# State-space mixer of an encoder block: plain fp32 products and VectorE power tables in place of split operands and GpSimd

## The chip, the cores and the metric

The kernel runs on one core of a Trainium2 chip. The metric is the device time of one launch in microseconds (us). The core has five engines with an instruction queue each: TensorE (PE; its weight loads are listed as PEld), VectorE (DVE), ScalarE (ACT), GpSimd (POOL) and SyncE (SP), which here only issues DMAs.

## The reference, cut to what matters

The program is one encoder block: RMSNorm, an input projection into a Fourier branch, a state-space branch and two gate vectors, a merge, and a mixture of experts. The change touches the state-space branch alone. For 32 groups of 16 channels and both directions it computes, with 64 complex states per group:

```
    lam = lax.complex(a_re.astype(jnp.float32), a_im.astype(jnp.float32))
    dt = jnp.exp(log_dt.astype(jnp.float32))[:, None]
    a_bar = jnp.exp(lam * dt)
    b_mat = lax.complex(b_re.astype(jnp.float32), b_im.astype(jnp.float32))
    b_bar = ((a_bar - 1.0) / lam)[..., None] * b_mat
    bu = jnp.einsum('blgc,gnc->blgn', ug.astype(jnp.complex64), b_bar)
    a = jnp.broadcast_to(a_bar, bu.shape)
    _, h = lax.associative_scan(_scan_combine, (a, bu), axis=1, reverse=reverse)
    c_mat = lax.complex(c_re.astype(jnp.float32), c_im.astype(jnp.float32))
    return jnp.einsum('blgn,gcn->blgc', h, c_mat).real
...
    y = y.reshape(b, l, SSM_WIDTH) + d_skip.astype(jnp.float32) * uf
    y = jax.nn.gelu(y)
```

The rest of the block is the same in both kernels.

## The kernel before, in words

The program runs in stages: input projection (`stage_a`), Fourier branch (`stage_f`), gates with the state-space branch (`stage_s`), merge and routing (`stage_m`), experts (`stage_e`) and a last sum (`stage_z`). This document is about `stage_s`.

The 2048 positions are cut into 256 blocks of 8. Within a block the recurrence is written as matrix products; from block to block a scan carries the state. The 32 groups are handled in 16 chunks of two groups (`CG = 2`), and a chunk `c` passes these steps:

- `prep(c)` builds `win`, the products of the input matrix `bb` with eight powers of the transition (`pw_w`); `prep_cy(c)` builds `cy` from the output matrix `cc` and powers `pw_c`; `prep_tab(c)` builds `tab`, a table of 256 rotations, as the product of two tables of 16. All three are complex outer products. In the kernel before they are done by `cmulp` (L599 to L605) on GpSimd: two multiplications (L602, L603), a subtraction (L604) and an addition (L605) for each group.
- `kern(c)` transposes `win` on TensorE (L986) into PSUM and splits it (`winT`).
- `toeplitz(c)` makes the kernel of the block in PSUM (L998 to L1001), ACT copies it out and sends it through DRAM (`kd`); `load_toep(c)` reads it back as a Toeplitz matrix (`toep`).
- `states(c)` multiplies `winT` with the input `u` into `ps` (L1026), and ACT copies the result to `sx` (L1029).
- `scan(c)`, on VectorE: rotate (L1041 to L1044), four scans over 256 blocks (L1048), rotate back (L1049 to L1052).
- `enter(c)` puts the scanned states, shifted by one block, into `hs`.
- `result(c)` sums three products in PSUM (`py`): `toep` with `u`, and two of `cy` with `hs`. The moving `hs` is read with a step of two elements (`"p (c h) -> p h c"`).
- `gelu(c)`: L1077 to L1093 and two stores.

A product with split operands is `mm3` (L56 to L61): each operand is a high part and a low part in the reduced fp32 format (`fp32r`), and three matmuls add high by high, low by high and high by low. `split` (L50 to L54) makes the parts: a cast on ACT (L53) and a subtraction on VectorE, or on GpSimd for `cyp` (L54).

The gate products fill TensorE between the steps. There are 64 gate units; a unit is 24 matmuls of 512 columns (`pg`, eight times `mm3`), a Tanh on ACT (L831), in half of the units a VectorE instruction (L833), and a store (L836). The Python generator `gates` emits a unit at every `g(1)`, and `split_w` makes the weights' parts (`wg_h` on ACT, `wg_l` on VectorE) some units ahead. The order of instructions on each engine is the order in which the code is written (the schedule is manual), so an engine's queue is in order: an instruction that waits holds up everything behind it. SyncE issues loads and stores in the same fashion. `gt_t`, the tile that takes a gate unit out of PSUM, has two buffers, so a unit's Tanh needs the store of the unit before last to have landed.

The loop over chunks (L1129 to L1155) runs, for chunk `c`: `states(c+1)`, `scan(c+1)`, one gate unit, `result(c)`, `kern(c+2)`, the split of `u`, `toeplitz(c+1)`, the first part of `gelu(c)`, `prep(c+3)`, one gate unit, the split and the building of `cy`, `load_toep(c+1)`, `enter(c+1)`, the rest of `gelu(c)`, `prep_tab(c+3)`, and the remaining gate units (one or two). With 16 chunks it takes most of the stage.

Of the kernel before, what the change touches and what calls it, by code (L numbers as in the profile page):

```python
# [36 lines left out]
class K:  # L37
# [640 lines left out]
    def ssm_setup(self, tp):  # L678
# [80 lines left out]
        A.copy(self.pw_w[f], pw[f, :, 0:8])  # L759
        A.copy(self.pw_w[r], pw[r, :, 7::-1])  # L760
        A.copy(self.pw_c[f], pw[f, :, 1:9])
        A.copy(self.pw_c[r], pw[r, :, 8:0:-1])
# [113 lines left out]
    def stage_s(self):  # L876
# [61 lines left out]

        def prep(c):
# [9 lines left out]
            win = s["win"] = p1.tile([P, 2, CG, 8, 16], F32, name="win")  # L949

            def weights(o, pw, m):
                tw = [t[:, :, :, 0:128].rearrange("p q g (s c) -> p q g s c", s=8) for t in temps()]
                for g in range(CG):
                    a = m[:, :, CG * c + g].unsqueeze(2).to_broadcast([P, 2, 8, 16])
                    w = tuple(pw[:, q : q + 1, :, CG * c + g].unsqueeze(3).to_broadcast([P, 2, 8, 16]) for q in range(2))
                    self.cmulp(GP, o[:, :, g], a, w, tuple(t[:, :, g] for t in tw))
# [4 lines left out]
        def prep_tab(c):
            if c >= N:
                return
            s = st[c]
            tr = [t.rearrange("p q g (a b) -> p q g a b", a=16) for t in temps()]
            tab = s["tab"] = p2.tile([P, 2, CG, 256], F32, name="tab")
            for g in range(CG):
                a = self.rot[0][:, :, CG * c + g].unsqueeze(2).to_broadcast([P, 2, 16, 16])
                w = tuple(self.rot[1][:, q : q + 1, CG * c + g].unsqueeze(3).to_broadcast([P, 2, 16, 16]) for q in range(2))
                self.cmulp(GP, tab[:, :, g].rearrange("p q (a b) -> p q a b", a=16), a, w, tuple(t[:, :, g] for t in tr))  # L970

        def prep_cy(c):
            if c < N:
                cy = st[c]["cy"] = p1.tile([P, 2, CG, 8, 16], F32, name="cy")
                st[c]["weights"](cy, self.pw_c, self.cc)

        def kern(c):
# [4 lines left out]
            winT = s["winT"] = self.pair(p1, [P, 2, CG, P], "winT")
            pk = psk.tile([P, 2, CG, P], F32, name="pw", tag="pk")
            for q in range(2):
                for g in range(CG):
                    nc.tensor.transpose(pk[:, q, g], s["win"][:, q, g].rearrange("p s c -> p (s c)"), self.ident)  # L986
# [1231 lines left out]
```

## Time and profile before

| what | us |
|---|---|
| median of 3 runs | 2553.9 (2549.96 to 2554.51) |
| the profiled execution, its own time | 2549.1 |
| span of the profiled execution | 2547.2 |
| PE busy in the span | 2328.8 (91%) |
| DVE busy | 2188.3 (86%) |
| ACT busy | 1389.3 (55%) |
| POOL busy | 1240.8 (49%) |

How to read it: times are us from the start of the span. "Busy" for PE counts matmuls to their modelled ends, which overlap the next matmul's start, so the pace of matmuls is read from start to start. The state-space chunks run from about 330 to 785 us of the span; the experts take the second half of the program, from about 1240 us on. In the rows, `m` stands for the tiles `m1` and `m2`, `u` and `toep` for `u0` and `toep0`.

### The profile page before, as it was taken

What the parts mean: (1) busy time and instruction counts of PE and PEld (TensorE: products, weight loads), DVE (VectorE), ACT (ScalarE), POOL (GpSimd) and SP (SyncE); (2) the same over time, 40 slices, a digit from 0 to 9 for tenths busy, and PEclk for the clock granted to TensorE, in tenths of its full rate; (3) what the DMA queues carried; (4) which work ended last, traced back from release to release, by engine and by line L of the source; (5) the groups of instructions that cost most, each with busy time, mean ns of one, the idle gap of its engine ahead of it and who ended that gap; (6) DMA issues with size and microseconds to landing.
All of it is one profiled execution on the core that took longest, in us unless ns stands there. A gap on an engine that the chain in (4) does not pass through costs nothing.

```text
span 2547.2 us, 33067 instructions
## 1 busy us (share of the span) xinstructions
PE 2328.8 (91%) x11930; PEld 1935.9 (76%) x11930; DVE 2188.3 (86%) x2816; ACT 1389.3 (55%) x1680; POOL 1240.8 (49%) x755
## 2 busy tenths in 40 slices
PE   6998988998899899999799997999999999999974
PEld 6996766777778799997677776777777777777752
DVE  7776699998993645556799998999999999999998
ACT  4443344544444322222577775777777777777731
POOL 2223898999960200012332462256565565655434
PEclk9999999999999999999799998999999999999985
DMA  5566624253335533326799988999999999989982
GB/s 193 183 195 236 222 88 142 79 187 120 118 97 157 180 109 100 116 76 231 257 335 374 366 314 351 369 355 350 356 354 369 363 360 378 375 339 344 359 324 115
DMA packets 201409, 632.75 MB, mean 248 GB/s; under 512 B 28998, under 2 KB 99656, under 8 KB 150556
## 3 DMA queue, kind: packets, MB, share of 16 engines
q1 hardware_dynamic: 170668, 571.01, 62.0%
q0 software_dynamic: 23104, 47.06, 4.9%
q10 hardware_dynamic: 7472, 12.55, 1.6%
q8 instruction: 94, 1.54, 0.2%
q14 instruction: 71, 0.58, 0.1%
HBM read 560.75 MB, written 103.32 MB: 261 GB/s over the span
## 4 chain that ended last, share of the span: by engine, by line
DVE 43%; PE 25%; issue 13%; POOL 11%; DMA 4%; ACT 2%; SPq 1%; DVEq 0%; POOLq 0%; ACTq 0%
DVE w_l L1715 21%; POOL t4a L602 3%; DVE xn L1853 3%; DVE xT_l L1794 3%; POOL t4b L603 3%; PE po L59 2%; PE po L61 2%; PE po L60 2%; DVE xg L1819 2%; DVE a L1893 2%; DVE aT_l L1794 1%; DVE a L1864 1%; PE pg L61 1%; PE pg L59 1%; PE pg L60 1%
## 5 line engine op out<-in xcount | busy, mean ns | idle before, releaser
L1715 DVE TENSOR_TENSOR w_l<-raw,w_h 128x2048 fp32r<-128x2048 f32 x384 | 868.5, 2292 | 12.7 <-ACT w_h L1709 12.7
L1709 ACT CAST w_h<-raw 128x2048 fp32r<-128x2048 f32 x384 | 726.4, 1906 | 206.4 <-PE pgu L61 162.1
L59 PE MATMUL pgu<-w_h,xT_h 128*128 128x512 f32 x1024 | 407.8, 398 | 14.0 <-issue 14.0
L60 PE MATMUL pgu<-w_l,xT_h 128*128 128x512 f32 x1024 | 408.4, 399 | 5.0 <-DVE w_l L1715 2.3
L61 PE MATMUL pgu<-w_h,xT_l 128*128 128x512 f32 x1024 | 402.7, 393 | 0.0
L1782 POOL DMA_INDIRECT y<-xg,ix x42 | 221.6, 5276 | 363.1 <-DVE aT_l L1794 326.0
L60 PEld LDWEIGHTS pgu<-w_l,xT_h 128*128 128x128 f32 x1024 | 194.2, 190 | 65.3 <-DVE w_l L1715 28.2
L59 PEld LDWEIGHTS pgu<-w_h,xT_h 128*128 128x128 f32 x1024 | 194.4, 190 | 53.6 <-issue 14.2
L61 PEld LDWEIGHTS pgu<-w_h,xT_l 128*128 128x128 f32 x1024 | 194.1, 190 | 39.7 <-DVE xT_l L1794 0.2
L1782 POOL DMA_INDIRECT y<-x_l,ix x22 | 114.9, 5221 | 205.6 <-DVE aT_l L1794 198.1
L61 PE MATMUL pg<-hk_h,wg_l 128*128 128x512 f32 x512 | 204.3, 399 | 10.3 <-DVE wg_l L54 10.3
L59 PE MATMUL pg<-hk_h,wg_h 128*128 128x512 f32 x512 | 207.6, 405 | 3.5 <-ACT gt_t L831 3.1
L59 PE MATMUL py<-w_h,aT_h 128*128 128x512 f32 x512 | 205.6, 402 | 4.0 <-ACT aT_h L1792 4.0
L60 PE MATMUL pg<-hk_l,wg_h 128*128 128x512 f32 x512 | 204.6, 400 | 0.0
L61 PE MATMUL py<-w_h,aT_l 128*128 128x512 f32 x512 | 200.4, 391 | 0.0
L60 PE MATMUL py<-w_l,aT_h 128*128 128x512 f32 x512 | 200.2, 391 | 0.0
L1777 POOL DMA_INDIRECT xg<-x,ix x42 | 176.1, 4193 | 12.8 <-issue 12.8
L1353 POOL TENSOR_TENSOR inv<-mv,mhalf 128x1 f32<-128x1 f32 x16 | 9.0, 560 | 239.3 <-DVE mv L1352 239.3
L61 PEld LDWEIGHTS pg<-hk_h,wg_l 128*128 128x128 f32 x512 | 99.4, 194 | 33.4 <-DVE wg_l L54 11.9
L59 PEld LDWEIGHTS pg<-hk_h,wg_h 128*128 128x128 f32 x512 | 99.7, 195 | 24.9 <-ACT gt_t L831 3.7
L60 PEld LDWEIGHTS pg<-hk_l,wg_h 128*128 128x128 f32 x512 | 99.6, 195 | 19.9
L59 PEld LDWEIGHTS py<-w_h,aT_h 128*128 128x128 f32 x512 | 96.7, 189 | 22.3 <-ACT aT_h L1792 4.2
(584 smaller groups left out, 5677.4 us busy)
## 6 DMA issues: line engine op xcount, KB each, us to landing
raw<-in_w_e SPq DMA_DIRECT2D x376, 1024.0 KB
wg_raw<-in_w_g SPq DMA_DIRECT2D x32, 512.0 KB
raw<-y SPq DMA_DIRECT2D x10, 1024.0 KB
hTh<-hp_h SPq DMA_DIRECT2D x8, 1024.0 KB
hTl<-hp_l SPq DMA_DIRECT2D x8, 1024.0 KB
hk_h<-hTh SPq DMA_DIRECT2D x16, 512.0 KB
hk_l<-hTl SPq DMA_DIRECT2D x16, 512.0 KB
yf<-yt SPq DMA_DIRECT2D x16, 512.0 KB
```

The source lines that it names most:

```text
L59: mm(out, a.h, b.h, start=start, stop=False)
L60: mm(out, a.h, b.l, start=False, stop=False)
L61: mm(out, a.l, b.h, start=False, stop=stop)
L602: tt(out=t[0], in0=a, in1=b[0], op=OP.mult)
L603: tt(out=t[1], in0=a[:, ::-1], in1=b[1], op=OP.mult)
L1709: self.nc.scalar.copy(self.ws[n].h, self.raws[n][0])
L1715: self.nc.vector.tensor_tensor(out=w.l, in0=raw, in1=w.h.bitcast(F32), op=OP.subtract)
L1777: self.nc.gpsimd.indirect_dma_start(out=xg, out_offset=None, in_=self.x2, in_offset=bass.IndirectOffsetOnAxis(ap=ix[:, e, 0:1], axis=0), b ...
L1782: self.nc.gpsimd.indirect_dma_start(out=self.y01, out_offset=bass.IndirectOffsetOnAxis(ap=ix[:, e, 1:2], axis=0), in_=r, in_offset=None, b ...
L1794: self.nc.vector.tensor_tensor(out=xT.l[:, k0 : k0 + 4], in0=ps, in1=xT.h[:, k0 : k0 + 4].bitcast(F32), op=OP.subtract)
L1819: self.nc.vector.scalar_tensor_tensor(x[:, ns], yo[n], tb[:, e, 2:3], x[:, ns], op0=OP.mult, op1=OP.add)
L1853: V.scalar_tensor_tensor(xn[s], xg, tb[:, s, 3:4], self.g2, op0=OP.mult, op1=OP.mult)
```

## The change: what it does

The products of the state-space branch take plain fp32 operands: `mm3` gives way to one `matmul` on fp32 tiles at `states` and `result`, and the splits of `u`, `winT`, `cy`, `toep` and `hs` go. A plain copy on ACT stays where a tile is moved (`winT` out of PSUM, `hs`). The outer products go from GpSimd to VectorE, by a new function `outer`: the power tables `pw_w`, `pw_c` and `rot[1]` get a third part, the negated imaginary part, written once by ACT, so that the subtraction and the addition at the end become one addition over both groups. `u` and `cy` get three buffers, `winT` and `toep` two. The loop's order changes: `prep_cy(c+2)` stands before `scan(c+1)`, and `prep_tab` builds two chunks ahead instead of three, behind `enter`.

```diff
-        self.pw_w, self.pw_c, self.rho = t("pw_w", [2, 8, G]), t("pw_c", [2, 8, G]), t("rho")
+        self.pw_w, self.pw_c, self.rho = t("pw_w", [3, 8, G]), t("pw_c", [3, 8, G]), t("rho")
...
+        for m in (self.pw_w, self.pw_c, self.rot[1]):
+            A.mul(m[:, 0], m[:, 2], -1.0)
...
-                u = st[c]["u0"] = p1.tile([P, CG, 2, P], F32, name="u0")
+                u = st[c]["u"] = p3.tile([P, CG, 2, P], F32, name="u")
...
-        def split_u(c):
-            if c < N:
-                u = st[c]["u"] = self.pair(p2, [P, CG, 256], "u")
-                self.split(u, st[c]["u0"].rearrange("p g h c -> p g (h c)"))
...
+        def outer(o, a, b, c, k, n):
+
+            w = 2 * k * n
+            m = [self.s_tmp.tile([P, CG, 512], F32, name=f"t4{q}", tag="sg" + q)[:, :, 0:w] for q in "ab"]
+            for g in range(CG):
+                x = a[:, :, CG * c + g]
+                y = b(CG * c + g)
+                for v, p, q in ((m[0], x, y[:, 1:2]), (m[1], x[:, ::-1], y[:, 0::2])):
+                    p = p.unsqueeze(2).to_broadcast([P, 2, k, n])
+                    q = (q.to_broadcast([P, 2, k]) if q.shape[1] == 1 else q).unsqueeze(3).to_broadcast([P, 2, k, n])
+                    V.tensor_tensor(out=v[:, g].rearrange("p (q k n) -> p q k n", q=2, k=k), in0=p, in1=q, op=OP.mult)
+            V.tensor_tensor(out=o.rearrange("p g q c -> p g (q c)"), in0=m[0], in1=m[1], op=OP.add)
...
-            weights(win, self.pw_w, self.bb)
-            s["weights"] = weights
+            outer(win, self.bb, lambda g: self.pw_w[:, :, :, g], c, 8, 16)
...
-                self.cmulp(GP, tab[:, :, g].rearrange("p q (a b) -> p q a b", a=16), a, w, tuple(t[:, :, g] for t in tr))
...
+                outer(tab, self.rot[0], lambda g: self.rot[1][:, :, g], c, 16, 16)
...
-            self.split(winT, pk)
+            A.copy(winT, pk)
...
-                    self.mm3(ps[:, q], s["winT"][:, q, g], s["u"][:, g], True, True)
+                    nc.tensor.matmul(ps[:, q], s["winT"][:, g, q], s["u"][:, g].rearrange("p h c -> p (h c)"), start=True, stop=True)
...
-                self.split(hs[fl, g, :, 1:257], m1[fl, g])
-                self.split(hs[bl, g, :, 0:255], m1[bl, g, :, 254::-1])
+                A.copy(hs[fl, g, :, 1:257], m1[fl, g])
+                A.copy(hs[bl, g, :, 0:255], m1[bl, g, :, 254::-1])
...
-                self.mm3(py[:, g], s["toep"][:, g], s["u"][:, g], True, False)
+                nc.tensor.matmul(py[:, g], s["toep"][:, g], s["u"][:, g].rearrange("p h c -> p (h c)"), start=True, stop=False)
                 for q in range(2):
-                    h = Pair(*(m[:, g, q, 0:256].rearrange("p (c h) -> p h c", h=2) for m in (hs.h, hs.l)))
-                    self.mm3(py[:, g], s["cyp"][:, q, g], h, False, q == 1)
+                    h = hs[:, g, q, 0:256].rearrange("p (c h) -> p h c", h=2)
+                    nc.tensor.matmul(py[:, g], s["cy"][:, g, q], h, start=False, stop=q == 1)
...
             states(c + 1)
+            prep_cy(c + 2)
             next(rest, None)
...
             kern(c + 2)
-            split_u(c + 2)
             toeplitz(c + 1)
             rest = gelu(c)
             next(rest)
             prep(c + 3)
             g(1)
-            split_cy(c + 1)
-            prep_cy(c + 2)
             load_toep(c + 1)
             enter(c + 1)
-            split_toep(c + 1)
+            prep_tab(c + 2)
             next(rest)
-            prep_tab(c + 3)
             g(n - 2)
```

On VectorE, behind the scan of a chunk, this stood before (the splits of `hs` and `toep` between the two parts of the GELU, L1078 and L1084):

```order
L1078 TENSOR_SCALAR ga<-ga 128x512
L1079 TENSOR_TENSOR ga<-ga,py 128x512
L833 SCALAR_TENSOR_TENSOR gt_t<-gt_t,gt_y 128x512
L54 TENSOR_TENSOR hs_l<-m_4017,hs_h 64x2x256
L54 TENSOR_TENSOR hs_l<-m_4017,hs_h 64x2x255
L54 TENSOR_TENSOR hs_l<-m_4017,hs_h 64x2x256
L54 TENSOR_TENSOR hs_l<-m_4017,hs_h 64x2x255
L54 TENSOR_TENSOR toep_l<-toep_4180,toep_h 128x256
L1084 SCALAR_TENSOR_TENSOR ygt<-ga,py 128x2x128
L1085 SCALAR_TENSOR_TENSOR ygt<-ga,py 128x2x128
```

In the changed kernel the same place ends with the last of the `win` instructions, a gate unit's VectorE instruction (now L836) and the rotation table:

```order
L935 TENSOR_TENSOR win<-t4a,t4b 128x512
L836 SCALAR_TENSOR_TENSOR gt_t<-gt_t,gt_y 128x512
L934 TENSOR_TENSOR t4a<-rot_2626,rot_2627 128x512
L934 TENSOR_TENSOR t4b<-rot_2626,rot_2627 128x512
L934 TENSOR_TENSOR t4a<-rot_2626,rot_2627 128x512
L934 TENSOR_TENSOR t4b<-rot_2626,rot_2627 128x512
L935 TENSOR_TENSOR tab<-t4a,t4b 128x1024
L1068 SCALAR_TENSOR_TENSOR ygt<-ga,py 128x2x128
L1069 SCALAR_TENSOR_TENSOR ygt<-ga,py 128x2x128
```

So five subtractions went, and between the two parts of the GELU now stand the five instructions of `win` and the five of `tab`. The third table, `cy`, stands on VectorE ahead of the scan, where before there was only the gate units' instruction:

```order
L54 TENSOR_TENSOR wg_l<-wg_raw,wg_h 128x1024
L836 SCALAR_TENSOR_TENSOR gt_t<-gt_t,gt_y 128x512 x2
L934 TENSOR_TENSOR t4a<-cc,pw_c 128x256
L934 TENSOR_TENSOR t4b<-cc,pw_c 128x256
L934 TENSOR_TENSOR t4a<-cc,pw_c 128x256
L934 TENSOR_TENSOR t4b<-cc,pw_c 128x256
L935 TENSOR_TENSOR cy<-t4a,t4b 128x512
L1025 TENSOR_TENSOR m_3910<-sx,tab 128x1024
```

The scan's first instruction (L1025, before L1041) thereby stands behind the gate unit's instruction and the five of `cy`. On TensorE, `result(c)` of one group was this:

```order
L59 MATMUL py<-u_h,toep_h 128x256
L60 MATMUL py<-u_l,toep_h 128x256
L61 MATMUL py<-u_h,toep_l 128x256
L59 MATMUL py<-hs_h,cyp_h 128x256
L60 MATMUL py<-hs_l,cyp_h 128x256
L61 MATMUL py<-hs_h,cyp_l 128x256
L59 MATMUL py<-hs_h,cyp_h 128x256
L60 MATMUL py<-hs_l,cyp_h 128x256
L61 MATMUL py<-hs_h,cyp_l 128x256
```

and of both groups, with the transposes behind it, it is now this:

```order
L1050 MATMUL py<-u,toep 128x256
L1053 MATMUL py<-hs,cy 128x256 x2
L1050 MATMUL py<-u,toep 128x256
L1053 MATMUL py<-hs,cy 128x256 x2
L970 MATMUL pw<-ident,win 128x128 x4
```

Nine matmuls on `fp32r` parts became three on plain fp32; the place among the gate units stays.

## Rows read from the trace of the kernel before

**Rows 1.** Busy time of each engine in stretches of the span (from:to, its length, then busy us of PE, PEld, DVE, ACT, POOL with instruction counts, the granted clock of TensorE as a share of full speed, the DMA share and GB/s): the start of the state-space chunks, all of them, a part of them, and one chunk from its first `ps` product to the next chunk's.

```profile
295.00:330.00 35.00, 34.32 (x172) 27.96 (x171) 20.10 (x21) 15.04 (x32) 31.62 (x40) 1.00 0.62 208
330.00:785.00 455.00, 403.93 (x2007) 331.19 (x2006) 415.88 (x409) 210.61 (x446) 394.74 (x362) 0.94 0.37 117
400.00:600.00 200.00, 183.79 (x903) 148.67 (x902) 186.08 (x179) 100.66 (x215) 195.01 (x180) 0.92 0.42 135
518.40:542.10 23.70, 23.70 (x128) 19.86 (x126) 20.50 (x19) 12.79 (x28) 23.15 (x22) 1.00 0.42 132
```

**Rows 2.** The chain of work that ended last, by line, of the stretch 400 to 575 us and of the stretch 575 to 700 us.

```profile
by line: POOL t4a L602 27.2%; POOL t4b L603 25.2%; issue 8.1%; POOL tab L605 8.1%; POOL tab L604 7.9%; POOL cy L605 6.9%; POOL cy L604 5.5%; POOL win L605 5.3%; POOL win L604 5.2%; DMA wg_raw<-in_w_g 2.1%; POOL cyp_l L54 0.2%; POOLq L604 0.
...
by line: issue 12.8%; DMA mf<-gt_t 12.1%; DVE sx L1048 11.3%; DVE gt_t L833 6.7%; DVE wg_l L54 5.6%; DVE m L1050 5.4%; ACT sx L1029 5.0%; DVE m L1042 5.0%; DVE m L1041 4.7%; DVE m L1049 4.5%; DVE m L1052 4.4%; DVE hs_l L54 3.5%; DVE m L1043
```

**Rows 3.** Who waited for whom from 330 to 785 us: total us, times, the longest.

```profile
ACT gt_t L831 <- DMA mf<-gt_t: 41.7, 10, 13.7
...
POOL cyp_l L54 <- ACT cyp_h L53: 26.7, 4, 13.4
PE ps L60 <- DVE u_l L54: 25.4, 4, 9.7
...
PE pg L61 <- DVE wg_l L54: 10.3, 3, 5.2
```

**Rows 4.** TensorE's timeline from 518 us on, one chunk: start, us, line and operation. Left out are the rest of the 12 `ps` products, of the gate units' `pg`, of the 18 `py` products and of the table products.

```profile
518.41 0.28 PE L59 MATMUL ps<-u_h,winT_h 128*128 128x256 f32 x1
518.53 0.28 PE L60 MATMUL ps<-u_l,winT_h 128*128 128x256 f32 x1
...
519.83 0.40 PE L59 MATMUL pg<-hk_h,wg_h 128*128 128x512 f32 x1
...
525.29 0.28 PE L59 MATMUL py<-u_h,toep_h 128*128 128x256 f32 x1
...
528.52 0.41 PE L61 MATMUL py<-hs_h,cyp_l 128*128 128x256 f32 x1
528.75 0.62 PE L986 MATMUL pw<-ident,win 128*128 128x128 f32 x4
...
531.10 0.50 PE L59 MATMUL pg<-hk_h,wg_h 128*128 128x512 f32 x1
...
542.10 0.28 PE L59 MATMUL ps<-u_h,winT_h 128*128 128x256 f32 x1
```

**Rows 5.** The first of the three matmul lines of the gate units, from 330 to 785 us: how many, busy us, mean ns of one, idle before.

```profile
L59 PE MATMUL pg<-hk_h,wg_h 128*128 128x512 f32 x394 | 160.5, 407 | 0.8 <-ACT gt_t L831 0.8
```

**Rows 6.** TensorE's timeline around a product of plain fp32 operands with 256 columns, in `stage_a` (L170). The profile lists two records for this one matmul.

```profile
143.85 0.28 PE L61 MATMUL pz<-hp_h,ws_l 128*128 128x256 f32 x1
143.97 0.59 PE L170 MATMUL pn<-sq,ones 128*128 128x256 f32 x2
144.21 0.47 PE L59 MATMUL pa<-wa_h,S_h 128*128 128x260 f32 x1
144.52 0.28 PE L60 MATMUL pa<-wa_l,S_h 128*128 128x260 f32 x1
```

**Rows 7.** VectorE groups by line and shape from 330 to 785 us, while GpSimd works: count, busy us, mean ns of one, idle before.

```profile
L1048 DVE TENSOR_TENSOR_SCAN sx<-rho,m 128x256 f32<-128x256 f32 x64 | 60.4, 1002 | 0.0
...
L54 DVE TENSOR_TENSOR wg_l<-wg_raw,wg_h 128x1024 fp32r<-128x1024 f32 x26 | 41.0, 1575 | 2.6 <-ACT wg_h L53 2.6
...
L54 DVE TENSOR_TENSOR hs_l<-m,hs_h 64x512 fp32r<-64x512 f32 x32 | 34.2, 1068 | 2.0 <-ACT hs_h L53 1.6
...
L833 DVE SCALAR_TENSOR_TENSOR gt_t<-gt_t,gt_y 128x512 f32<-128x512 f32 x26 | 27.3, 1071 | 9.8 <-ACT gt_t L831 9.8
...
L54 DVE TENSOR_TENSOR toep_l<-toep,toep_h 128x256 fp32r<-128x256 f32 x16 | 12.7, 792 | 1.8 <-ACT toep_h L53 1.5
```

**Rows 8.** VectorE's timeline in the last chunk, when GpSimd has no tables left to build.

```profile
753.71 0.41 DVE L1084 SCALAR_TENSOR_TENSOR ygt<-ga,py 128x256 f32<-128x256 f32 x1
754.04 0.41 DVE L1085 SCALAR_TENSOR_TENSOR ygt<-ga,py 128x256 f32<-128x256 f32 x1
754.37 1.21 DVE L54 TENSOR_TENSOR wg_l<-wg_raw,wg_h 128x1024 fp32r<-128x1024 f32 x1
755.50 1.21 DVE L1041 TENSOR_TENSOR m<-sx,tab 128x1024 f32<-128x1024 f32 x1
756.64 1.21 DVE L1042 TENSOR_TENSOR m<-sx,tab 128x1024 f32<-128x1024 f32 x1
757.89 0.69 DVE L1043 TENSOR_TENSOR m<-m,m 128x512 f32<-128x512 f32 x1
758.50 0.69 DVE L1044 TENSOR_TENSOR m<-m,m 128x512 f32<-128x512 f32 x1
759.10 2.43 DVE L1048 TENSOR_TENSOR_SCAN sx<-rho,m 128x256 f32<-128x256 f32 x4
...
764.57 0.69 DVE L1052 SCALAR_TENSOR_TENSOR m<-m,m 128x512 f32<-128x512 f32 x1
766.45 0.43 DVE L1078 TENSOR_SCALAR ga<-ga 128x512 f32<-128x512 f32 x1 [1.20 <-ACT ga L1077]
766.99 0.69 DVE L1079 TENSOR_TENSOR ga<-ga,py 128x512 f32<-128x512 f32 x1
```

**Rows 9.** VectorE's timeline at the start of the chunk of rows 4: its wait for the copies of `sx` behind the `ps` products.

```profile
521.94 1.23 DVE L1041 TENSOR_TENSOR m<-sx,tab 128x1024 f32<-128x1024 f32 x1 [3.06 <-issue]
```

More of the change, by code (lines that the diff above doesn't have):

```diff
@@ L684, in ssm_setup @@
         self.bb, self.cc = new("bb", [2, G, 16]), new("cc", [2, G, 16])
-        self.rot = [new(f"rot{q}", [2, G, 16]) for q in range(2)]
+        self.rot = [new("rot0", [2, G, 16]), new("rot1", [3, G, 16])]
         tt, ts = V.tensor_tensor, V.tensor_scalar
         t = lambda n, shape=[G]: tp.tile([P] + shape, F32, name=n)
-        self.pw_w, self.pw_c, self.rho = t("pw_w", [2, 8, G]), t("pw_c", [2, 8, G]), t("rho")
+        self.pw_w, self.pw_c, self.rho = t("pw_w", [3, 8, G]), t("pw_c", [3, 8, G]), t("rho")
         are, aim, ldt = t("are"), t("aim"), t("ldt")
@@ L758, in ssm_setup @@
         f, r = slice(0, 64), slice(64, 128)
[L759 to L762, printed above, removed]
+        A.copy(self.pw_w[f, 1:3], pw[f, :, 0:8])
+        A.copy(self.pw_w[r, 1:3], pw[r, :, 7::-1])
+        A.copy(self.pw_c[f, 1:3], pw[f, :, 1:9])
+        A.copy(self.pw_c[r, 1:3], pw[r, :, 8:0:-1])
+        for m in (self.pw_w, self.pw_c, self.rot[1]):
+            A.mul(m[:, 0], m[:, 2], -1.0)
         yield
@@ L895, in stage_s @@
         cx = self.s_cx
-        p1, p2 = self.pool(cx, "s_p1", 1, "right"), self.pool(cx, "s_p2", 2, "right")
+        p1, p2, p3 = (self.pool(cx, f"s_p{n}", n, "right") for n in (1, 2, 3))
         pss = self.pool(cx, "s_pss", 2, space=PSUM)
@@ L948, in prep @@
                 A.copy(b[q][bl, :, 32:48], src[bl, gs])
[L949 to L956, printed above, removed]
-            weights(win, self.pw_w, self.bb)
-            s["weights"] = weights
-        def prep_tab(c):
[L962 to L969, printed above, removed]
-                self.cmulp(GP, tab[:, :, g].rearrange("p q (a b) -> p q a b", a=16), a, w, tuple(t[:, :, g] for t in tr))
+            win = s["win"] = p1.tile([P, CG, 2, P], F32, name="win")
+            outer(win, self.bb, lambda g: self.pw_w[:, :, :, g], c, 8, 16)
+        def prep_tab(c):
+            if c < N:
+                tab = st[c]["tab"] = p2.tile([P, CG, 2, 256], F32, name="tab")
+                outer(tab, self.rot[0], lambda g: self.rot[1][:, :, g], c, 16, 16)
         def prep_cy(c):
             if c < N:
-                cy = st[c]["cy"] = p1.tile([P, 2, CG, 8, 16], F32, name="cy")
-                st[c]["weights"](cy, self.pw_c, self.cc)
+                cy = st[c]["cy"] = p3.tile([P, CG, 2, P], F32, name="cy")
+                outer(cy, self.cc, lambda g: self.pw_c[:, :, :, g], c, 8, 16)
         def kern(c):
@@ L981, in kern @@
             s = st[c]
[L982 to L986, printed above, removed]
-            self.split(winT, pk)
+            winT = s["winT"] = p2.tile([P, CG, 2, P], F32, name="winT")
+            pk = psk.tile([P, CG, 2, P], F32, name="pw", tag="pk")
+            for g in range(CG):
+                for q in range(2):
+                    nc.tensor.transpose(pk[:, g, q], s["win"][:, g, q], self.ident)
+            A.copy(winT, pk)
         def toeplitz(c):
@@ L997, in toeplitz @@
                 for q in range(2):
-                    nc.tensor.matmul(pk[:, g, 16:144], b[q][:, g], s["cy"][:, q, g].rearrange("p s c -> p (s c)"), start=q == 0, stop=q == 1)
+                    nc.tensor.matmul(pk[:, g, 16:144], b[q][:, g], s["cy"][:, g, q], start=q == 0, stop=q == 1)
                 for q, src in enumerate((self.bb[:, 0], nbb)):
@@ L1012, in load_toep @@
             s = st[c]
-            toep = s["toep0"] = p1.tile([P, CG, P], F32, name="toep0")
+            toep = s["toep"] = p2.tile([P, CG, P], F32, name="toep")
             for g in range(CG):
@@ L1036, in scan @@
             sx = s["sx"]
-            ct, sn = (s["tab"][:, q].unsqueeze(2).to_broadcast([P, CG, 2, 256]) for q in range(2))
+            ct, sn = (s["tab"][:, :, q].unsqueeze(2).to_broadcast([P, CG, 2, 256]) for q in range(2))
             m1 = s["m1"] = p1.tile([P, CG, 2, 256], F32, name="m1")
@@ L1098, in stage_s @@
         load_u(0)
+        load_u(1)
         prep(0)
+        prep_tab(0)
         prep_cy(0)
-        prep_tab(0)
         g(first - 2)
         kern(0)
-        split_u(0)
         V.tensor_tensor(out=dd, in0=dd, in1=self.ident[0:16, 0:16].unsqueeze(1).to_broadcast([16, G, 16]), op=OP.mult)
-        load_u(1)
         g(1)
```

25 lines of the change are left out of this document (5 added, 20 removed).

## The prediction, made before the changed kernel was run

> **What bounds the kernel now.** The change touches the state-space chunks only, so I began with busy time by stretch [rows 1]. From 330 to 785 us 16 chunks run, 28.4 us each. POOL is busy 195.01 of the 200 us between 400 and 600, DVE 186.08, PE 183.79: three engines look full at once. The chain of waits says which one ends last [rows 2]: from 400 to 575 us nearly all of it is GpSimd's outer products (t4a and t4b alone are over half). From 575 to 700 us it is DVE's scan and rotations, mixed with the landing of the gate stores. The list of waits [rows 3] shows how this reaches TensorE: 25.4 us for u_l, a subtraction that stands in DVE's queue behind the scan, 10.3 us for wg_l, and ACT stands 41.7 us for a free gt_t buffer, whose store waits on a late DVE instruction.
>
> Is TensorE a floor close below? The chunk from 518.41 to 542.10 has no gap: PE is busy all 23.70 us at full clock, with three gate units in it [rows 1, 4]. Its parts, start to start: 12 ps products 1.42 us, a gate unit 5.46, the 18 py products 3.46, transposes and table products 2.35. The 394 first-line matmuls [rows 5] at 8 per unit are 49.25 units, 3.08 per chunk, so the mean chunk needs 23.7 + 0.08 x 5.46 = 24.1 us of TensorE. Sixteen need 386 us where 455 were taken. The 69 us between are waits (455 - 404 = 51 us idle) and matmuls at the lower clock (mean granted clock 0.94 in that stretch, of the levels 1.2 and 2.4 GHz).
>
> **The change, part by part.**
>
> TensorE. A split product is three matmuls of 256 columns, 0.118 us apart (518.41 to 518.53) [rows 4], so 0.354. A plain fp32 one of the same size stands between the steps at 143.97 and about 144.40 (the next step, 144.52, less one of 0.12) [rows 6]: 0.43 us. The four ps products go from 1.42 to 1.72 us, the two of toep from 0.71 to 0.86. The four of hs are read with a step of two. Split, they are 0.23 us apart (528.52 to 528.75), twice the packed pace: 12 x 0.23 = 2.75 us. No row shows a plain fp32 product with such an operand. From below it costs the packed 0.43; from above the same doubling, 0.43 x 0.23 / 0.118 = 0.84. Its two records take 0.215 each for 256 columns, already about the 0.23 at which the step-two operand arrives, so I take 2 x 0.23 = 0.46, or 1.84 us for four. Sum: +0.30 + 0.15 - 0.91 = -0.46 us a chunk (upper end +0.45 + 0.61 = +1.1). The mean chunk then needs 23.6 us of TensorE, 378 for sixteen.
>
> Here a page of the Trainium skill speaks against the change: "FP8 and Floating Point Precision", section "TensorE Precision Notes", has true fp32 as four passes through the array. The packed rows agree: 0.43 against 0.354 is more than three passes cost. Another page, "SBUF — State Buffer", section "Door 1: The DMA port swizzle", holds that fp32 may be strided while two reads still hit one 16-byte line, so a step of two would be free; the trace differs, 0.23 against 0.118. By that page alone the hs products would cost 0.43 each, by the doubling 0.84.
>
> VectorE. It loses the subtractions of hs (four, 1.07 us each), toep (0.79) [rows 7], u and winT. It gains 15 instructions a chunk: for win and for cy four multiplications of 256 elements and one addition of 512, for tab four of 512 and one of 1024. No row shows outer products on DVE. When GpSimd is quiet, instructions of these sizes follow each other at 0.33 us (753.71 to 754.04), 0.60 (758.50 to 759.10) and 1.14 us (755.50 to 756.64) [rows 8]. That gives 4 x 0.33 + 0.60 = 1.92 twice, and 4 x 0.60 + 1.14 = 3.54: 7.4 us. From above, the toep subtraction beside a busy GpSimd took 0.79 for 256 elements and the hs one 1.07 for 512 [rows 7]: 8 x 0.79 + 6 x 1.07 + 2.3 (1.14 doubled) = 15.0 us. I take 7.4, since GpSimd has nothing left to do there and that is the state of rows 8. The same makes everything else on DVE cheaper: one scan instruction 0.61 us (2.43 for four) against 1.0, the scan block 755.50 to 765.26 = 9.8 us. The whole chunk: 9.8, GELU 1.8 (0.54 + 0.60 + 0.67), tables 7.4, wg_l 1.6 x 1.14, gate instruction 1.6 x 0.60 (26 of each over 16 chunks [rows 7]): 21.8 us, against 415.88 / 16 = 26.0 before.
>
> The order on DVE adds a chain. cy stands behind the gate instruction, which needs the chunk's last gate unit, and the scan needs sx, 3.5 us after the first ps product (518.41 to 521.94) [rows 4, 9]. cy and the gate instruction, 2.5 us, fit into that wait. Behind it: 9.8 + 1.14 + 1.14 + 1.92 + 0.60 + 3.54 + 0.67 + 1.14 + 0.60 = 20.6, together 24.1 us in a chunk that has everything. That is level with TensorE, so in those chunks little slack is left; in chunks whose gates need no DVE instruction about a microsecond more.
>
> ACT and queues. ACT loses the casts of u, cy and toep, keeps a copy for each other cast, and had 210.61 of 455 us busy: no term. On SP the load of u no longer waits for a split. GpSimd's tables go off the path whole. The start (295 to 330 us) has PE busy 34.32 of 35 us: moving its tables gains nothing there; DVE had 15 us idle to take the first 7.4. One chunk builds win in buffers that also hold the zeros for clearing a table in DRAM; DVE may wait there once; that is counted in the waits kept below.
>
> Sum: TensorE 23.6 us a chunk. Not all waits go: store landings, the level DVE chain, and clock lost after each gap. Before, these and GpSimd cost 69 / 16 = 4.3 us a chunk; I keep a third, 1.4. So 25.0 us, 400 instead of 455: -55. Later stages are untouched and follow at the same distance. Against the profiled execution's 2549.1 (span 2547.2) that is 2494; the median of runs is 4.8 above it, so 2499.
>
> **The rivals.**
>
> *Step-two fp32 products pay twice.* TensorE goes to 24.1 + 1.1 = 25.2, with 1.4 of waits 26.6 us: 426, -29, so 2525. For it: the split rows doubled. Against: the pace of the two records. By the four-pass rule each pass would be strided; no run here shows it.
>
> *DVE's queue ends last.* If the 15 instructions cost 10 us (short, with broadcast operands and more overhead than rows 8), the full chunk's chain is 24.1 + 2 = 26 and with waits about 27: 432, -23, so 2531. For it: the level sums, and DVE busy in rows 1. Against: setup products with broadcasts run on DVE beside these at the usual pace.
>
> *Slower than before.* If strided and broadcast operands put all 15 at the upper end, 15.0 us, that is twice the price: 5.5 us more behind the scan and 1.0 of cy that the wait for sx no longer covers, 30.6 in a full chunk, about 29.8 in the mean one, over the 28.4 of now: 16 x 1.4 = +22, so 2576. It decides from about 13 us of tables a chunk. Against: what slowed those rows is gone.
>
> *Nothing left but TensorE.* 23.6 us flat: 378, -77, so 2477. For it: the chunk of rows 4 had no gap. Against: not one in three chunks was like it.
>
> **How the numbers follow.** Forecast 0.62 (its own range 2484 to 2514, waits between 0.5 and 2.3 us a chunk), strided products 0.16, DVE's queue 0.10, slower 0.05, floor 0.07. The range from 2477 to 2533 leaves out the slower case and the outer edges of the floor and queue cases, about 0.13. What three runs can tell from no change is 0.2%, 5 us: faster by more 0.92, within it 0.03, slower 0.05.
>
> **What would show it.** Right: first ps product to the next chunk's about 25 us, GpSimd near zero there, granted clock above 0.94, scan instructions near 0.61 us start to start, the wait of ps for u_l gone, chain made of TensorE. py products of hs at 0.46 us settle the first rival, t4a multiplications of 256 elements at 0.33 us the second and third. Wrong: DVE gapless through the chunks, or a wait of pg for wg_l or gt_t that stays near the 50 us of now.

## The result and the profile after

The changed kernel took 2483.0 us (median; 2478.0 to 2485.6), the kernel before, run beside it, 2554.2. The ratio is 0.9722, with a 95% interval of 0.9704 to 0.9741: 71 us or 2.8% faster. The forecast was 2499 us, a gain of 55; the likeliest case was right in kind and 16 us too small, and 2483.0 lies just below the range that it gave itself (2484 to 2514).

The page of the profile after, engine by engine:

```profile
PE 2304.4 (93%) x11770; PEld 1914.1 (77%) x11770; DVE 2111.1 (85%) x2944; ACT 1367.5 (55%) x1635; POOL 722.2 (29%) x354
```

The view of busy time by stretch answers to [rows 1]. The columns are the same: busy us of PE, PEld, DVE, ACT, POOL, then the granted clock, the DMA share and GB/s. The chunks now end near 715 us instead of 785.

```profile
295.00:330.00 35.00, 32.27 (x127) 26.14 (x126) 21.61 (x36) 9.62 (x20) 0.00 (x0) 0.88 0.61 208
330.00:715.00 385.00, 383.16 (x1902) 312.58 (x1902) 338.66 (x525) 193.51 (x410) 0.53 (x1) 1.00 0.45 142
400.00:600.00 200.00, 199.08 (x999) 162.28 (x998) 176.40 (x276) 102.87 (x223) 0.00 (x0) 1.00 0.48 153
```

PE is idle 1.84 of 385 us and its clock is granted in full. Before, it stood 51 us idle in the chunks at a mean of 0.94. GpSimd is gone from them. VectorE has 338.66 us of work where it had 415.88. The first line, the start, shows a loss: PE has 32.27 us at a clock of 0.88, where it had 34.32 at 1.00.

The chain that ended last, 330 to 715 us, answers to [rows 2]:

```profile
by line: PE pg L59 15.8%; PE pg L61 15.4%; PE pg L60 15.2%; PE py L1053 4.7%; PE ps L1010 4.3%; DVE sx L1032 3.7%; PE pkk L982 2.9%; issue 2.8%; DVE t4b L934 2.5%; DVE t4a L934 2.5%; DMA hk_h<-hTh 2.3%; PE py L1050 2.3%; DMA mf<-gt_t 2.1%; 
```

GpSimd's outer products were over half of it from 400 to 575 us, and no GpSimd row is left. It is now mostly the matmuls of the gate units (pg). The waits, 325 to 715 us, answer to [rows 3]: the waiting engine and line, its releaser, us in total, times, the longest.

```profile
ACT gt_t L834 <- DMA mf<-gt_t: 33.5, 7, 8.6
...
DVE m L1025 <- ACT sx L1013: 11.5, 4, 4.7
...
PE pg L61 <- DVE wg_l L54: 1.8, 2, 0.9
```

The 25.4 us of ps for u_l are gone with the subtraction. Of the 10.3 us of pg for wg_l, 1.8 stay. ACT still stands 33.5 us for store landings, yet PE hardly stands at all.

One chunk on TensorE, from 512.06 us, answers to [rows 4]. Now a row has several records; two belong to one plain product.

```profile
512.06 1.89 PE L1010 MATMUL ps<-u,winT 128*128 128x256 f32 x8
513.60 0.58 PE L59 MATMUL pg<-hk_h,wg_h 128*128 128x512 f32 x1
514.02 0.39 PE L60 MATMUL pg<-hk_l,wg_h 128*128 128x512 f32 x1
...
519.25 0.60 PE L1050 MATMUL py<-u,toep 128*128 128x256 f32 x2
519.68 1.07 PE L1053 MATMUL py<-hs,cy 128*128 128x256 f32 x4
520.59 0.60 PE L1050 MATMUL py<-u,toep 128*128 128x256 f32 x2
521.02 1.08 PE L1053 MATMUL py<-hs,cy 128*128 128x256 f32 x4
521.94 0.60 PE L970 MATMUL pw<-ident,win 128*128 128x128 f32 x4
```

Read start to start, the four ps products end where the first pg begins in earnest, one pg pace (0.23) before 514.02, so 1.73 us; a toep product takes 519.68 - 519.25 = 0.43 us, two hs products 520.59 - 519.68 = 0.91, so 0.455 each.

VectorE by form, 330 to 715 us, answers to [rows 7] (count, busy us, mean ns of one, idle before):

```profile
L1032 DVE TENSOR_TENSOR_SCAN sx<-rho,m 128x256 f32<-128x256 f32 x64 | 38.9, 671 | 0.0
L54 DVE TENSOR_TENSOR wg_l<-wg_raw,wg_h 128x1024 fp32r<-128x1024 f32 x26 | 31.7, 1220 | 6.0 <-ACT wg_h L53 6.0
L934 DVE TENSOR_TENSOR t4a<-rot,rot 128x512 f32<-128x512 f32 x30 | 20.6, 686 | 0.1
...
L934 DVE TENSOR_TENSOR t4a<-cc,pw_c 128x256 f32<-128x256 f32 x30 | 12.6, 419 | 0.0
...
L1063 DVE TENSOR_TENSOR ga<-ga,py 128x512 f32<-128x512 f32 x15 | 10.3, 688 | 1.6
```

The same scan instruction went from a mean of 1002 ns to 671 with GpSimd quiet, wg_l from 1575 to 1220. The outer products, which no row showed before, have the durations of plain instructions of their size.

To measure a chunk I take first ps product to first ps product. The timelines give 335.61 and 751.78 us for chunks 1 and 15 before, 343.86 and 682.64 after: a mean of 29.73 and of 24.20 us over 14 steps. These steps hold 44 gate units in both kernels, 3.14 each, a little more than the 3.08 of all chunks. After, TensorE's work for that is 23.25 + 0.14 x 5.4 = 24.0, so that 0.2 us a step are waits. From chunk 1's ps to the last py (the start of its row, which holds four records after), the loop took 448.1 us before (335.61 to 783.73) and 368.8 after (343.86 to 712.67). Below, "the loop" is that stretch, and "the start" is the time from the issue of the last store to yf (`yf<-row`, which ends the stage ahead) to the first ps product: 314.27 - 279.96 = 34.3 us before, 323.32 - 283.61 = 39.7 after.

### The profile page after: what moved, and what is told of

It is laid out like the page before. It is cut to its first block, busy times and chain, and to the rows that moved or that the text cites. A ratio compares the mean times of both kernels' runs of the same rounds, so it can differ in the third digit from the quotient of the medians.

```text
span 2481.1 us, 32354 instructions
## 1 busy us (share of the span) xinstructions
PE 2304.4 (93%) x11770; PEld 1914.1 (77%) x11770; DVE 2111.1 (85%) x2944; ACT 1367.5 (55%) x1635; POOL 722.2 (29%) x354
## 4 chain that ended last, share of the span: by engine, by line
DVE 41%; PE 36%; issue 12%; DMA 6%; ACT 3%; POOL 1%; SPq 1%; DVEq 0%; POOLq 0%; ACTq 0%
DVE w_l L1691 19%; PE pg L59 3%; PE pg L61 3%; PE pg L60 3%; DVE xT_l L1770 3%; DVE xn L1829 2%; PE po L59 2%; PE pgu L60 2%; PE po L61 2%; PE po L60 2%; PE pgu L61 2%; PE pgu L59 2%; DVE xg L1795 2%; DVE a L1869 2%; ACT w_h L1685 2%
## 5 line engine op out<-in xcount | busy, mean ns | idle before, releaser
L1758 POOL DMA_INDIRECT y<-xg,ix x42 | 180.7, 4302 | 423.3 <-DVE aT_l L1770 386.2
L1758 POOL DMA_INDIRECT y<-x_l,ix x22 | 94.4, 4292 | 235.6 <-DVE aT_l L1770 228.2
L1753 POOL DMA_INDIRECT xg<-x,ix x42 | 156.9, 3735 | 12.8 <-issue 12.8
L61 PEld LDWEIGHTS py<-w_h,aT_l 128*128 128x128 f32 x512 | 96.7, 189 | 20.8 <-DVE aT_l L1770 0.3
```

Of the source, the lines that this page charges most:

```text
L61: mm(out, a.l, b.h, start=False, stop=stop)
L1753: self.nc.gpsimd.indirect_dma_start(out=xg, out_offset=None, in_=self.x2, in_offset=bass.IndirectOffsetOnAxis(ap=ix[:, e, 0:1], axis=0), b ...
L1758: self.nc.gpsimd.indirect_dma_start(out=self.y01, out_offset=bass.IndirectOffsetOnAxis(ap=ix[:, e, 1:2], axis=0), in_=r, in_offset=None, b ...
```

## The experiments

Two questions stood open. Which of the change's halves (tables off GpSimd, products without splits) brings the gain, and through what? And what sets the pace now, so that a gain of TensorE alone or of VectorE alone could still count? The runs of the first four stand against 2556.9 us of before, those of the last four against 2554.5, and the change against 2554.2; so a difference in us between runs of two of these sets is good to some 3 us.

| run | us | ratio to before, 95% | loop, us | start, us |
|---|---|---|---|---|
| before, profiled beside the change | 2554.2 | | 448.1 | 34.3 |
| the change | 2483.0 | 0.9704 to 0.9741 | 368.8 | 39.7 |
| e1, tables back on GpSimd | 2529.4 | 0.9868 to 0.9901 | 425.0 | 34.8 |
| e2, tables moved, splits kept | 2559.2 | 0.9999 to 1.0018 | 449.1 | 42.9 |
| e3, idle work on GpSimd | 2634.3 | 1.0285 to 1.0321 | 514.8 | 50.2 |
| e4, first tables later | 2474.5 | 0.9655 to 0.9687 | 372.7 | 34.2 |
| e5, tab products twice | 2512.3 | 0.9805 to 0.9849 | 398.3 | 44.1 |
| e6, ps products twice | 2502.8 | 0.9777 to 0.9828 | 393.1 | 41.3 |
| e7, ps split again, on e4 | 2484.6 | 0.9703 to 0.9753 | 377.5 | 34.4 |
| e8, hs packed, on e4 | 2475.7 | 0.9666 to 0.9708 | 369.7 | 35.0 |

**e1: the tables back on GpSimd, products plain.**

```diff
-                    V.tensor_tensor(out=v[:, g].rearrange("p (q k n) -> p q k n", q=2, k=k), in0=p, in1=q, op=OP.mult)
-            V.tensor_tensor(out=o.rearrange("p g q c -> p g (q c)"), in0=m[0], in1=m[1], op=OP.add)
+                    GP.tensor_tensor(out=v[:, g].rearrange("p (q k n) -> p q k n", q=2, k=k), in0=p, in1=q, op=OP.mult)
+            GP.tensor_tensor(out=o.rearrange("p g q c -> p g (q c)"), in0=m[0], in1=m[1], op=OP.add)
```

> The changed kernel with its 15 outer-product instructions a chunk issued on GpSimd instead of VectorE; plain fp32 products stay. Theory A (GpSimd's outer products ended last before; with them gone TensorE alone sets the pace): GpSimd's price by the rows of before lies between its shortest (4 x 0.64 + 1.1 twice, 4 x 1.05 + 2.0: about 13.5 us a chunk) and its mean (about 23 us without cyp); near the upper end the chunk is 24 to 25 us and the kernel 10 to 30 us slower than the changed one, 2495 to 2515. Rival B (the gain is the split operands that went, wherever the tables are built): the same as the changed kernel, 2483 within 5.

Measured: 2529.4, 28 us faster than before and 46 slower than the change: neither expectation came, and the loss is above the upper end of theory A (2515). Stretch 400 to 600 us, two of GpSimd's groups there, one of VectorE's and a wait of PE:

```profile
400.00:600.00 200.00, 184.60 (x905) 149.95 (x904) 151.07 (x134) 93.64 (x203) 157.90 (x123) 0.97 0.44 144
```

```profile
L934 POOL TENSOR_TENSOR t4a<-rot,rot 128x512 f32<-128x512 f32 x18 | 29.4, 1632 | 0.7
...
L935 POOL TENSOR_TENSOR win<-t4a,t4b 128x512 f32<-128x512 f32 x8 | 14.1, 1762 | 39.0 <-PE pw L970 38.9
...
L54 DVE TENSOR_TENSOR wg_l<-wg_raw,wg_h 128x1024 fp32r<-128x1024 f32 x12 | 23.3, 1942 | 1.2 <-ACT wg_h L53 1.2
...
PE pg L61 <- DVE wg_l L54: 15.4, 2, 10.1
```

GpSimd is not full (157.90 of 200; it waits 38.9 us for TensorE's transposes), and neither is VectorE (151.07). What the rows show instead are longer instructions on both: a multiplication of 512 elements takes 1632 ns there and 686 on VectorE, wg_l beside it has a mean of 1942 ns, and PE waits 15.4 us for wg_l in this stretch. So with the tables left on GpSimd the rest of the change is worth some 28 us, and where the tables stand matters still. That rest is the removal of the splits together with the new order, the added buffers and 15 table instructions a chunk in place of 24; no run takes these apart.

**e2: the tables on VectorE, products split as before.**

```diff
-                    self.cmulp(GP, o[:, :, g], a, w, tuple(t[:, :, g] for t in tw))
+                    self.cmulp(V, o[:, :, g], a, w, tuple(t[:, :, g] for t in tw))
...
-                self.cmulp(GP, tab[:, :, g].rearrange("p q (a b) -> p q a b", a=16), a, w, tuple(t[:, :, g] for t in tr))
+                self.cmulp(V, tab[:, :, g].rearrange("p q (a b) -> p q a b", a=16), a, w, tuple(t[:, :, g] for t in tr))
```

> The kernel before with only the tables moved to VectorE (24 cmulp instructions a chunk there), split products kept. VectorE then has 9.8 scan + 4.6 gates and GELU + 3.9 subtractions + 7.9 tables = 26 us a chunk at the quiet prices. Theory A: VectorE ends last instead of GpSimd, 26 to 27 us a chunk, so 15 to 35 us faster than before: 2520 to 2540. Rival B (the splits that went are the gain): no gain or slower, 2550 and up.

Measured: no gain at all, 2559.2 against 2556.9; the expected 2520 to 2540 failed.

```profile
400.00:600.00 200.00, 177.90 (x897) 146.84 (x896) 195.85 (x357) 95.61 (x207) 11.03 (x7) 0.93 0.43 139
```

VectorE has 195.85 of 200 us: it has taken GpSimd's place as the full engine [rows 1]. So the halves don't add: 28 us for the one, nothing for the other, 71 for both. The splits' subtractions had to leave VectorE to make room for the tables. How much room the new function `outer` made, no run shows: e2 keeps the old loop order and builds its tables with 24 instructions a chunk, where the change has 15.

**e3: the change, and beside each outer product on VectorE eight multiplications on GpSimd, of the sizes that it did before, into a tile that nobody reads.**

```diff
+            x, y = (m.rearrange("p q g s -> p (q g s)") for m in (self.cc, self.bb))
+            for _ in range(2):
+                for w in (2 * k * n, 2 * k * n, k * n, k * n):
+                    GP.tensor_tensor(out=ns[:, 0:w], in0=x[:, 0:w], in1=y[:, 0:w], op=OP.mult)
```

> The changed kernel, and GpSimd does beside it as many multiplications of the same sizes as the tables took before, on scratch that nobody reads. Theory C (the busy GpSimd slowed VectorE's instructions, and that was a good part of the loss): VectorE's scan goes from 0.61 to about 1.0 us and its chunk from about 21 to 28 us or more, so the kernel is 60 to 90 us slower than the changed one, 2545 to 2575. Theory A without it: scan instructions slower but TensorE still sets the pace, 2483 to 2495.

Measured: 2634.3, 151 us slower than the change and 77 slower than before, for work on which nothing waits. Stretch 400 to 600 us, and three of VectorE's groups in it:

```profile
400.00:600.00 200.00, 152.14 (x690) 121.09 (x691) 197.92 (x188) 70.29 (x154) 181.38 (x168) 0.87 0.30 96
```

```profile
L1043 DVE TENSOR_TENSOR_SCAN sx<-rho,m 128x256 f32<-128x256 f32 x24 | 26.7, 1169 | 0.0
...
L945 DVE TENSOR_TENSOR t4a<-rot,rot 128x512 f32<-128x512 f32 x10 | 11.4, 1137 | 0.1
...
L1074 DVE TENSOR_TENSOR ga<-ga,py 128x512 f32<-128x512 f32 x5 | 3.4, 688 | 0.5
```

A scan of 671 ns takes 1169 here, a multiplication of 686 ns 1137 (over all chunks 1014 and 1004), and VectorE is full with fewer instructions (188 against 276). That GpSimd slows VectorE is thereby shown, with nothing else changed; 60 to 90 us were expected of it. Not every instruction is slowed: ga<-ga,py, which reads one of its two inputs from PSUM, takes 688 ns here as in the change. The Trainium skill ("SBUF — State Buffer", section "Who interferes with whom") names one cause: a VectorE instruction with two inputs in SBUF contends with a GpSimd instruction that reads SBUF, over a shared pair of ports. The rows agree that these instructions contend, and those with an input in PSUM do not; that the ports are where it happens no run here shows.

**e4: the change, with the first chunk's tab and cy built behind the first gate units, instead of ahead of them.**

```diff
         prep(0)
-        prep_tab(0)
-        prep_cy(0)
         g(first - 2)
         kern(0)
+        prep_tab(0)
+        prep_cy(0)
```

> The changed kernel with the first chunk's tab and cy built behind the first gate units instead of ahead of them. If those 10 instructions at the start hold up the gate unit's instruction (308.90 us), SP's loads behind it and so TensorE: 3 to 6 us faster than the changed kernel, 2477 to 2480, and the first ps product 3 to 6 us earlier than 323.3. If the late start is the wait for gate weights from DRAM alone: no change, within 2 us.

Measured: 2474.5 (2473.3 to 2476.5), 8.5 us faster than the change, more than the 3 to 6 expected, and the best of all. VectorE's timeline in the change, with the gate instruction (gt_t) behind the tables, then SP's, and ACT's and PE's waits:

```profile
300.84 0.42 DVE L934 TENSOR_TENSOR t4a<-bb,pw_w 128x256 f32<-128x256 f32 x1
...
303.03 0.69 DVE L934 TENSOR_TENSOR t4a<-rot,rot 128x512 f32<-128x512 f32 x1
...
305.56 1.23 DVE L935 TENSOR_TENSOR tab<-t4a,t4b 128x1024 f32<-128x1024 f32 x1
306.82 0.43 DVE L934 TENSOR_TENSOR t4a<-cc,pw_c 128x256 f32<-128x256 f32 x1
...
308.29 0.69 DVE L935 TENSOR_TENSOR cy<-t4a,t4b 128x512 f32<-128x512 f32 x1
308.90 0.68 DVE L836 SCALAR_TENSOR_TENSOR gt_t<-gt_t,gt_y 128x512 f32<-128x512 f32 x1
```

```profile
309.61 0.34 SPq L829 DMA_DIRECT2D gt_y<-yf  x1
309.99 0.43 SPq L839 DMA_DIRECT2D mf<-gt_t  x1
310.53 0.38 SPq L802 DMA_DIRECT2D wg_raw<-in_w_g  x1
```

```profile
314.53 1.04 ACT L53 CAST wg_h<-wg_raw 128x1024 fp32r<-128x1024 f32 x1 [6.83 <-DMA wg_raw<-in_w_g]
...
316.12 0.50 PE L59 MATMUL pg<-hk_h,wg_h 128*128 128x512 f32 x1 [2.73 <-ACT gt_t L834]
```

In the change 8.1 us of tables (300.84 to 308.90) stand ahead of the gate instruction; e4 moves all but win behind it. The next load of gt_y can't be issued before it has run (309.61), and on SP's queue the weights' load (wg_raw) stands behind that one. ACT then waits 6.83 us for the weights and PE 2.73 us. In e4 the gate instruction runs at 301.96, and the start takes 34.2 us instead of 39.7 (34.4 and 35.0 in e7 and e8, which are built on e4, and 34.8 in e1, where GpSimd builds these tables):

```profile
301.96 0.68 DVE L836 SCALAR_TENSOR_TENSOR gt_t<-gt_t,gt_y 128x512 f32<-128x512 f32 x1
```

```profile
295.00:330.00 35.00, 35.00 (x166) 28.49 (x165) 26.04 (x42) 12.28 (x28) 0.00 (x0) 0.97 0.67 228
```

So 5.4 us of the start's 39.7 were the change's own, and e4 has them back. In e4's profiled execution the loop took 3.8 us more than in the change's: TensorE has two waits there that the change has not, on VectorE's wg_l and ahead of a py product.

```profile
403.84 0.50 PE L61 MATMUL pg<-hk_h,wg_l 128*128 128x512 f32 x1 [1.61 <-DVE wg_l L54]
...
587.40 0.67 PE L1050 MATMUL py<-u,toep 128*128 128x256 f32 x2 [1.67 <-issue]
```

So a net 1.7 of the 8.5 can be shown; what lies ahead of and behind this stretch is the same code, and the rest has no cause that I can name.

**e5: tab's multiplications twice**, for VectorE.

```diff
-                    V.tensor_tensor(out=v[:, g].rearrange("p (q k n) -> p q k n", q=2, k=k), in0=p, in1=q, op=OP.mult)
+                    for _ in range(1 + (k == 16)):
+                        V.tensor_tensor(out=v[:, g].rearrange("p (q k n) -> p q k n", q=2, k=k), in0=p, in1=q, op=OP.mult)
```

> The changed kernel, with the four multiplications of 512 elements of each tab table issued twice on VectorE: 2.4 us more a chunk there, nothing more on TensorE. Theory A (TensorE alone sets the pace of the chunks; VectorE had 338.66 of 385 us busy, 2.9 us a chunk free): the added work is hidden for the most part, 0 to +10 us over the changed kernel, 2483 to 2493 us. Theory B (VectorE's chain is level with TensorE in the full chunks, as the prediction had it, and any addition behind the scan shows): 16 x 2.4 = +38, about 2521 us.

**e6: each ps product twice**, for TensorE.

```diff
-                    nc.tensor.matmul(ps[:, q], s["winT"][:, g, q], s["u"][:, g].rearrange("p h c -> p (h c)"), start=True, stop=True)
+                    for _ in range(2):
+                        nc.tensor.matmul(ps[:, q], s["winT"][:, g, q], s["u"][:, g].rearrange("p h c -> p (h c)"), start=True, stop=True)
```

> The changed kernel, with each of the four ps products of a chunk done twice on TensorE (the second starts the sum anew, so the output is the same): 4 x 0.43 = 1.72 us more a chunk there, nothing more on the other engines. Theory A (TensorE sets the pace): the whole addition shows, 16 x 1.72 = +27.5 us, about 2510 us. Theory B (VectorE's chain sets it): less than half of it shows, under 2496 us.

Measured: e5 +29 us, e6 +20 over the change. The stretch 400 to 600 us of e5, then of e6:

```profile
400.00:600.00 200.00, 192.94 (x936) 155.88 (x935) 185.47 (x289) 95.67 (x207) 0.00 (x0) 0.97 0.45 146
```

```profile
400.00:600.00 200.00, 199.49 (x990) 163.58 (x990) 163.15 (x255) 94.93 (x203) 0.00 (x0) 1.00 0.42 137
```

First what was added. On VectorE it is more than the 2.4 us a chunk of the expectation, as e5's timeline shows beside the change's, where the same four multiplications take 305.56 - 303.03 = 2.53 us (the fence of e4):

```profile
347.75 1.42 DVE L935 TENSOR_TENSOR t4a<-rot,rot 128x512 f32<-128x512 f32 x2
...
353.18 1.23 DVE L936 TENSOR_TENSOR tab<-t4a,t4b 128x1024 f32<-128x1024 f32 x1
```

Doubled, they take 5.43, so 2.9 us more a chunk. In the loop, e5 shows 398.3 - 368.8 = 29.5 of its 15 x 2.9 = 43.5 us, e6 24.3 of 15 x 1.73 = 26. Neither theory holds alone. An addition on TensorE shows almost whole: PE is busy 199.49 of 200. An addition on VectorE shows for two thirds: what could be hidden was (43.5 - 29.5) / 15 = 0.9 us a chunk in the mean. It doesn't show evenly: of the fourteen steps, five are 4.2 to 8.9 us longer than in the change and the others within 0.3; in the loop TensorE waits 12.7 us ahead of py products and 7.5 for wg_l. Yet VectorE's busy time in the change left (385 - 338.66) / 16 = 2.9 us a chunk. Part of that idle time lies where the next work can't use it: VectorE waits for sx, ahead of its work ([rows 9], and 11.5 us in the waits after). The two engines are nearly level, as the prediction's sum for a full chunk had it.

**e7: e4 with the products of ps split again** (winT and u only).

```diff
-            A.copy(winT, pk)
+            self.split(winT, pk)
+            up = s["up"] = self.pair(p1, [P, CG, 256], "up")
+            self.split(up, s["u"].rearrange("p g h c -> p g (h c)"))
...
-                    nc.tensor.matmul(ps[:, q], s["winT"][:, g, q], s["u"][:, g].rearrange("p h c -> p (h c)"), start=True, stop=True)
+                    self.mm3(ps[:, q], s["winT"][:, g, q], s["up"][:, g], True, True)
```

> The kernel of e4_first_tables_later, with the products that make ps alone split again (winT and u into two parts each: two copies on ScalarE, two subtractions of 512 elements on VectorE a chunk, about 1.3 us): TensorE has 1.42 us instead of 1.72 for them. Theory A (TensorE sets the pace, VectorE has 2.9 us a chunk to spare): 16 x 0.30 = -5 us against that kernel, about 2470 us. Theory B (VectorE's chain is level, and the copies and subtractions stand ahead of ps again): 0 to +25 us, 2475 to 2500 us.

Measured: 2484.6, 10 us slower than e4: theory A's gain of 5 failed, and the time lies in theory B's range. TensorE's least chunk did shrink, to 22.96 us from 23.25 (483.62 to 506.58 there, 484.18 to 507.43 in e4), the expected 0.30. But the loop took 4.8 us more. VectorE's stretch 400 to 600 has 184.00 us where e4's has 174.29. TensorE's idle time in the chunks goes from 5.1 us to 11.1, 6.5 of them for wg_l, and ps waits for a subtraction again:

```profile
PE ps L60 <- DVE up_l L54: 1.9, 1, 1.9
```

So plain ps products cost TensorE 0.3 us a chunk and are still the better choice here. The waits speak for VectorE, which pays for a split; what the two further casts on ACT and the single buffers of the split parts add, no run takes apart.

**e8: e4 with hs stored packed**, so that the step of two stands in ACT's copies and not in the products.

```diff
-                A.copy(hs[fl, g, :, 1:257], m1[fl, g])
-                A.copy(hs[bl, g, :, 0:255], m1[bl, g, :, 254::-1])
+                A.copy(hs[fl, g, :, 1], m1[fl, g, :, 0::2])
+                A.copy(hs[fl, g, :, 0, 1:128], m1[fl, g, :, 1:255:2])
+                A.copy(hs[bl, g, :, 0], m1[bl, g, :, 254::-2])
+                A.copy(hs[bl, g, :, 1, 0:127], m1[bl, g, :, 253::-2])
...
-                    h = hs[:, g, q, 0:256].rearrange("p (c h) -> p h c", h=2)
+                    h = hs[:, g, q].rearrange("p h c -> p (h c)")
```

> The kernel of e4_first_tables_later, with hs stored so that its products read packed columns (the copies on ScalarE take the step of two instead, eight of 256 elements for four of 512). Theory A (the step costs a plain fp32 product 0.455 against 0.43 us): 4 x 0.025 x 16 = -1.6 us, about 2473 us, and the records of py<-hs,cy at 0.215 us each. Theory B (the step costs nothing, and 0.455 is the products' own order or the bank of py): the records stay at 0.227 us and the time within 1 us of 2474.5. Theory C (the eight strided copies delay the result): +5 us or more.

Measured: 2475.7, the same as e4 within what can be told; by the time alone theory B would have held. Its rows for the py products:

```profile
513.56 1.03 PE L1055 MATMUL py<-hs,cy 128*128 128x256 f32 x4
514.43 0.59 PE L1052 MATMUL py<-u,toep 128*128 128x256 f32 x2
```

Two products take 514.43 - 513.56 = 0.87 us packed, 0.91 with the step. By these rows the step costs a plain product 0.02 us, or 5%, and a whole chunk with three gate units takes 23.13 us instead of 23.25, which is 0.03 a product: theory A's 0.025 holds. Four products in each of 16 chunks make 1.3 to 1.9 us, too little to see in the time.

## Why the prediction was right, and where it was off

- **TensorE's sum.** Right to the hundredth. The prediction had 23.70 - 0.46 = 23.24 us for a chunk with three gate units; the timeline shows 23.25 (488.81 to 512.06). Its terms hold too: ps was taken at 1.72 and read at 1.73, which e6 confirms (342.33 to 367.31 us, 24.98 instead of 23.25 for a chunk with one set more); for hs 0.46 was taken and 0.455 measured.
- **Step-two products pay twice.** That rival falls: 0.455, not 0.84. By the Trainium skill ("SBUF — State Buffer", section "Door 1: The DMA port swizzle") fp32 reads may be strided as long as two of them fall on one 16-byte line. A step of two would then cost nothing: for the plain products this is nearly so (0.455 against 0.435 packed, e8), for the split ones it isn't [rows 4]. What I took, that the slow pace of plain products covers the step, fits both; the mechanism itself was not measured.
- **The tables on VectorE.** 7.4 us were taken; chunk 0's take 308.90 - 300.84 = 8.1 us start to start, since the addition comes some 0.1 us after the last multiplication and 1024 elements take 1.26 us there. Far from the 13 at which the slower case would begin. The upper bound of 15.0 us is what a busy GpSimd would have made of them: e3's rows, 1137 ns for 512 elements, come near it (the bound had 1.07 us for that size).
- **The quiet GpSimd.** The step "GpSimd has nothing left to do there and that is the state of rows 8" carried the whole forecast for VectorE, and e3 shows how much hung on it: 151 us.
- **The kept waits.** This is the term that was mis-sized: "I keep a third, 1.4" us a chunk. PE was idle 1.84 us in 385, about 0.1 a chunk, at full clock. The sixteen chunks thus gained 16 x 1.3 = 21 us more than forecast, and the waits fell out of the range of the likeliest case (0.5 to 2.3). The reason given for keeping them, the level chain of VectorE, is real (e5), but level is not late: in the mean VectorE had room for 0.9 us a chunk. In the chunks it is the rival with nothing left but TensorE (chance 0.07) that came: it had -77 us, and the loop took 79 less (448.1 to 368.8), against the -55 of the likeliest case. Its 2477 is also the nearest to the measured time. That the time still came close to the likeliest case's range is partly luck, as the next two points show.
- **The start.** "Moving its tables gains nothing there; DVE had 15 us idle to take the first 7.4" was the step that failed. The idle time was there, but the tables stand ahead of the gate instruction in VectorE's queue, and behind that instruction hung a load on SP, the weights, ACT's cast and PE: 5.4 us lost. The rule that the prediction used for the loop (what is queued behind) was not used here.
- **The sum.** Forecast -55, then -21 of waits that went and +5.4 of the start: -71, which is also what the medians differ by. That it closes so well is chance. In the two profiled executions the stretch from the last store to yf to the last py is 503.8 and 429.1 us, 75 shorter. What lies ahead of and behind it was 8.6 us longer in the later execution, with the same code; the experiments' profiled executions spread there by as much, and why is open.

## What to carry to other kernels

When three engines look equally full, moving work from one to another can only pass the bound on (e2); here it paid together with an edit that takes work off the engine that receives. For an engine that gets new work, busy time is not enough: find what stands behind it in that engine's queue, in the prologue as in the loop, and place the new work behind whatever releases a load or a store (e4). Where VectorE and GpSimd run side by side, price both from rows taken beside each other, since the same instruction took up to 1.7 times as long here.
